# Down projection of a SwiGLU block: six of eleven pairs of row blocks as Strassen-Winograd units between the gate products

## The chip, the cores and the metric

The kernel runs on one core of a Trainium2 chip. The metric is the time of one execution in device microseconds (us). Of the kernel before there are three runs, with a median of 1959.67 us (1958.75 to 1963.95), and one execution with a profile. The engines are called as in the profile: PE (TensorE, the matmuls), PEld (its weight loads), DVE (VectorE), ACT (ScalarE), POOL (GpSimd) and SP (SyncE, which issues the loads from DRAM).

## The reference

The program is an encoder of two layers (DEPTH 2) on 512 tokens with 1024 channels, all in float32. Each layer has a SwiGLU feed-forward block (FFN), a mixer of four kinds of attention heads, and a second FFN:

```python
def _swiglu(h, w_gu, w_down):
    gate, up = jnp.split(h @ w_gu, 2, axis=-1)
    return (jax.nn.silu(gate) * up) @ w_down
...
    alpha = (2 * DEPTH) ** 0.25
    for l in range(DEPTH):
        x = _layer_norm(alpha * x + 0.5 * _swiglu(x, ffn_w_gu[l, 0], ffn_w_down[l, 0]), ln_g[l, 0], ln_b[l, 0])
        mix = _token_mixers(x, ...)
        x = _layer_norm(alpha * x + mix, ln_g[l, 1], ln_b[l, 1])
        x = _layer_norm(alpha * x + 0.5 * _swiglu(x, ffn_w_gu[l, 1], ffn_w_down[l, 1]), ln_g[l, 2], ln_b[l, 2])
```

The inner width D_FF is 2816, so w_gu is 1024 x 5632 (gate and up side by side) and w_down is 2816 x 1024. There are four FFNs in all; only they are touched here, the mixers are not.

## The kernel before

**Precision.** A float32 operand is split into a high part (a cast by ACT to a matmul type, `wh`, `hh`) and a low part (the rest, a subtraction by DVE, `wl`, `hl`). Every product is three matmuls: high by high, high by low, low by high.

**Gate and up.** The work goes by eleven pairs j = 0 to 10 (class `Pair`). A pair makes 256 columns of the gate and the 256 columns of the up projection for all tokens, as a 2 x 2 block matrix product with seven products in place of eight (Winograd's form). Its four blocks of weights `b11`, `b21`, `b12`, `b22` (128 x 1024 each) are loaded by SP and added up to the operands of the seven products; the sums of the activations `al1` to `al7` stand ready for the whole FFN. Each operand of weights is split by `parts4` (the cast at L399, the low part at L400). One product (`product`, L404 to L416) is two halves of 12 matmuls with 256 columns. The program runs them in the order 1, 2, 5, 6, 7, 3, 4 into the PSUM tiles `ga` (1, 6, 7, 4), `gb` (2) and `gc` (5, 3); between them ACT copies intermediate results (`s1`, `p5`, `u2`) and DVE adds to them, and at the end of the pair silu and two multiplications give `h0` and `h1`, the pair's two blocks of 256 inner channels for the two halves of the tokens. In pairs 0 and 1 of an FFN the order is different: products 1 and 2 of both pairs come first, since the later products need the later token blocks, which the stage before has just finished.

`prep_rest` makes four sums of weights with DVE (L442): b11 + b12 in place, `t2` = b11 + b12 + b22 in a tile of its own, b12 + b22 in place, and b21 + t2 in place. For pair 0 these sums are made while the stage before still runs, since nothing holds them back but the loads.

**Down projection.** After the last pair come 22 row blocks c (128 inner channels each). A block's weights, 128 x 1024, are loaded (`wr`), cast and split (L237, L238), and its part of h is cast and split by `h_of` (L532, L533). For each of four token blocks and two column halves, `down` (L537) runs three matmuls of 512 columns, 24 for a row block. They accumulate in all eight PSUM banks (`acc`) from c = 0 to 21. The last four row blocks (TAIL) run token block by token block, so that the layer norm of one block goes on while the next is still computed. The layer norm reads a bank and adds it, times 0.5/alpha, to x (L313), where x is the residual.

**What sets the order.** The program is one stream per engine. The framework's scheduler places the instructions of each engine, within the dependencies; pools of tiles with a fixed number of buffers per tag set how early a load or a cast can start. `h` tiles live in free buffers of the mixers' tags (HSLOTS), since all 22 of them must be there until the down projection. `gain_later` (L358) multiplies x by the gain and adds the shift of the layer norm before, for the FFNs that follow one whose normalization was left so (FFNs 2 to 4); before, it runs after pairs 2, 3, 4 and 5, one token block at each.

Of the kernel before, what the change touches and what calls it, by code (L numbers as in the profile page):

```python
# [11 lines left out]
F32 = mybir.dt.float32  # L12
F32R = mybir.dt.float32r
# [59 lines left out]
def tile_encoder(ctx: ExitStack, tc: tile.TileContext, d: dict, out: bass.AP):  # L73
# [293 lines left out]
    HSLOTS = ["oT"] * 8 + ["nat"] * 4 + ["tb"] * 3 + ["hl"] * 6 + ["v"]  # L367
    TMP = ["o", "o", "od", "o2", "o2", "kr"]

    def ffn(l, f, last, to_next):  # L370
# [3 lines left out]
        slots = list(HSLOTS)  # L374
# [43 lines left out]
        class Pair:  # L418
# [16 lines left out]
            def prep12(self, early=(None, None)):  # L435
                self.w[1] = parts4(self.r[11], early[0])
                self.w[2] = parts4(self.r[21], early[1])
                return self

            def prep_rest(self):  # L440
                r = self.r
                add = lambda o, a, b: ve.tensor_tensor(o, a, b, op=ALU.add)  # L442
                add(r[11], r[11], r[12])
                self.w[5] = parts4(r[11])
                t2 = raw_tile("t2")
                add(t2, r[11], r[22])
                self.w[6] = parts4(t2)
                add(r[12], r[12], r[22])
                self.w[7] = parts4(r[12])
                self.w[3] = parts4(r[22])  # L450
                add(r[21], r[21], t2)
                self.w[4] = parts4(r[21])
                return self

# [3 lines left out]
            def run12(self):  # L458
                self.a = self.bank("s", "ga")
                product(1, self.a, self.w[1], True)  # L460
                self.s1 = tmp("s1").rearrange("p (c t) -> p c t", c=2)
                se.copy(self.s1, self.a)
                b = self.bank("pj", "gb")
                product(2, b, self.w[2], True)

                ve.tensor_tensor(self.s1, b, self.s1, op=ALU.add)

            def run_rest(self):
                v3 = lambda t: t.rearrange("p (c t) -> p c t", c=2)
                a = self.a  # L470
                c = self.bank("pj", "gc")
                product(5, c, self.w[5], True)
                p5 = v3(tmp("p5"))
                se.copy(p5, c)
                product(6, a, self.w[6], False)
                u2 = v3(tmp("u2"))
                se.copy(u2, a)  # L477
                product(7, a, self.w[7], False)

                ve.tensor_tensor(p5, a, p5, op=ALU.add)  # L480
                product(3, c, self.w[3], False)
                se.activation(self.s1, self.s1, AF.Silu, scale=-1.0)

                ve.tensor_tensor(u2, c, u2, op=ALU.add)
                product(4, a, self.w[4], False)
                h0 = v3(block(slots.pop(0), "h0"))
                ve.tensor_tensor(h0, self.s1, u2, op=ALU.mult)
                s2 = v3(tmp("s2"))
                se.activation(s2, a, AF.Silu, scale=-1.0)
                h1 = v3(block(slots.pop(0), "h1"))  # L490
                ve.tensor_tensor(h1, s2, p5, op=ALU.mult)
                H.append((h0, h1))

        p0, p1 = Pair(0), Pair(1)
        if opening:
            opening.pop(0)()
            p0.load().prep12(("p", "nat"))
            p0.run12()
            opening.pop(0)()
# [1061 lines left out]
```

## Time and profile before

| what | value |
|---|---|
| median of three runs | 1959.67 us |
| profiled execution | 1961.2 us, span 1959.4 us |
| granted TensorE clock, mean | 0.991 |
| FFN 1: gate and up, then down | 11.0 to 248.0 us, to about 369 |
| FFN 2 | 630.5 to 864.6, to about 988 |
| FFN 3 | about 989 to 1216, to about 1337 |
| FFN 4 | 1596 to 1831.4, to about 1951 |

The times of the four FFNs are the first and last starts of the tiles `ga` and `acc` in the trace. The mixers of the two layers lie between FFN 1 and 2 and between FFN 3 and 4. A group's row in the profile reads: line of the kernel, engine, operation, tile written and tile read, shapes, count, then the busy time in us and the mean duration of one in ns, then the idle time of the engine just before these instructions and what ended it. Window rows give for a stretch of time the busy time of PE, PEld, DVE, ACT and POOL with the number of instructions, the granted clock, the share of the DMA engines and GB/s.

### The profile page before, as it was taken

The numbers are of one execution on the slowest core, as the hardware profiler recorded it, in microseconds if no ns is written. First come the engines' busy times: TensorE is split into PE (matmuls) and PEld (weight loads), VectorE is DVE, ScalarE is ACT, GpSimd is POOL, SyncE is SP. The second block draws the span as 40 slices with busy tenths as digits, with TensorE's granted clock in tenths as the row PEclk, the third lists the DMA queues.
The fourth block names the chain that finished last, engine by engine and source line by source line (L and its number), as shares of the span: only waits on it lengthen the run. The fifth ranks groups of instructions, "written<-read, shape, count | busy, mean of one in ns | idle before, by whom it ended". The sixth has DMA issues, their size and how long they took to land. (4 is left out here: it accounts for less than half of the span.)

```text
span 1959.4 us, 32008 instructions
## 1 busy us (share of the span) xinstructions
PE 1905.6 (97%) x12396; PEld 1729.8 (88%) x12396; DVE 1452.8 (74%) x2265; ACT 999.1 (51%) x1695; POOL 262.4 (13%) x387
## 2 busy tenths in 40 slices
PE   7999999999999999999999999999999989999998
PEld 7999988788778899998899999887887879999886
DVE  7887753758999998763499787437689989978535
ACT  5544442238776754453275545322587875544421
POOL 0000000235741000000000000004367300000001
PEclk9999999999999999999999999999999999999999
DMA  5333233343333333332323322331433434332321
GB/s 192 114 103 97 97 115 104 100 113 87 107 101 105 113 103 104 108 129 97 103 90 111 110 96 99 108 120 55 134 90 84 107 100 141 99 108 85 108 97 65
DMA packets 157496, 205.61 MB, mean 105 GB/s; under 512 B 14560, under 2 KB 123104, under 8 KB 157344
## 3 DMA queue, kind: packets, MB, share of 16 engines
q1 hardware_dynamic: 157344, 203.56, 33.4%
q8 instruction: 98, 1.61, 0.3%
q14 instruction: 54, 0.44, 0.1%
HBM read 178.49 MB, written 2.10 MB: 92 GB/s over the span
## 5 line engine op out<-in xcount | busy, mean ns | idle before, releaser
L399 ACT CAST wh<-b 128x1024 fp32r<-128x1024 f32 x256 | 268.2, 1050 | 292.0 <-issue 168.9
L265 PE MATMUL ga<-al,wh 128*128 128x256 f32 x2752 | 392.1, 285 | 0.3 <-ACT u L477 0.3
L400 DVE TENSOR_TENSOR wl<-b,wh 128x1024 fp32r<-128x1024 f32 x256 | 310.3, 1218 | 93.4 <-ACT wh L399 93.3
L265 PEld LDWEIGHTS ga<-al,wh 128*128 128x128 f32 x2752 | 354.4, 191 | 8.9 <-ACT u L477 8.7
L238 DVE TENSOR_TENSOR wl<-wr,wh 128x1024 fp32r<-128x1024 f32 (+1 forms) x92 | 112.2, 1220 | 228.8 <-ACT wh L237 228.8
L265 PE MATMUL acc<-wl,hh 128*128 128x512 f32 x704 | 274.7, 390 | 0.0
L265 PE MATMUL acc<-wh,hl 128*128 128x512 f32 x704 | 274.3, 390 | 0.0
L265 PE MATMUL acc<-wh,hh 128*128 128x512 f32 x704 | 274.3, 390 | 0.0
L237 ACT CAST wh<-wr 128x1024 fp32r<-128x1024 f32 (+2 forms) x98 | 101.5, 1040 | 254.7 <-PE acc L265 219.8
L265 PE MATMUL ga<-al,wl 128*128 128x256 f32 x1376 | 221.3, 283 | 0.0
L333 POOL TENSOR_TENSOR rs<-rs,mhalf 128x1 f32<-128x1 f32 x24 | 20.0, 833 | 1481.3 <-DVE rs L332 1466.8
L265 PE MATMUL gc<-al,wh 128*128 128x256 f32 x1408 | 201.0, 285 | 5.9 <-ACT al L177 4.5
L265 PEld LDWEIGHTS ga<-al,wl 128*128 128x128 f32 x1376 | 189.7, 192 | 0.2 <-DVE wl L400 0.2
L265 PEld LDWEIGHTS gc<-al,wh 128*128 128x128 f32 x1408 | 183.6, 193 | 7.0 <-ACT al L177 4.8
L265 PEld LDWEIGHTS acc<-wl,hh 128*128 128x128 f32 x704 | 132.2, 188 | 28.0 <-DVE wl L238 0.5
L265 PEld LDWEIGHTS acc<-wh,hl 128*128 128x128 f32 x704 | 132.2, 188 | 27.1
L265 PEld LDWEIGHTS acc<-wh,hh 128*128 128x128 f32 x704 | 132.2, 188 | 26.9
L265 PE MATMUL gc<-al,wl 128*128 128x256 f32 x704 | 120.0, 284 | 0.0
L442 DVE TENSOR_TENSOR b<-b,b 128x1024 f32<-128x1024 f32 x88 | 107.2, 1219 | 2.6 <-DMA b<-in_ffn_w_gu_dram 1.7
L265 PE MATMUL gb<-al,wh 128*128 128x256 f32 x640 | 93.2, 289 | 9.2 <-ACT wh L399 9.2
L265 PEld LDWEIGHTS gc<-al,wl 128*128 128x128 f32 x704 | 100.6, 193 | 0.0
L265 PEld LDWEIGHTS gb<-al,wh 128*128 128x128 f32 x640 | 85.4, 198 | 9.6 <-ACT wh L399 9.6
(293 smaller groups left out, 3408.6 us busy)
## 6 DMA issues: line engine op xcount, KB each, us to landing
b<-in_ffn_w_gu_dram SPq DMA_DIRECT2D x176, 512.0 KB, 3.4
wr<-in_ffn_w_down_dram SPq DMA_DIRECT2D x88, 512.0 KB, 3.2
wr<-in_w_in_dram SPq DMA_DIRECT2D x30, 512.0 KB, 3.7
k<-ph SPq DMA_DIRECT2D x64, 128.0 KB, 2.4
wr<-in_w_out_dram SPq DMA_DIRECT2D x16, 512.0 KB, 3.3
qs<-ph SPq DMA_DIRECT2D x32, 128.0 KB, 2.4
ln_g<-in_ln_g_dram SPq DMA_DIRECT2D x14, 256.0 KB, 5.5
ln_b<-in_ln_b_dram SPq DMA_DIRECT2D x14, 256.0 KB, 5.8
```

The costliest lines, as they stand in the source:

```text
L237: se.copy(h[:, w], r[:, w])
L238: (lo or ve).tensor_tensor(l[:, q], r[:, q], h[:, q].bitcast(F32), op=ALU.subtract)
L265: te.matmul(o, a, b, start=start, stop=stop, **kw)
L333: ge.tensor_tensor(rs[:, 1:2], rs[:, 0:1], mhalf[:, 0:1], op=ALU.pow)
L399: se.copy(h, r[:, q])
L400: ve.tensor_tensor(lo, r[:, q], h.bitcast(F32), op=ALU.subtract)
L442: add = lambda o, a, b: ve.tensor_tensor(o, a, b, op=ALU.add)
```

## The change

Pairs 0 to 5, so row blocks 0 to 11 of the down weights, no longer go through the accumulating loop. Two pairs make a unit (class `Unit`, three per FFN): four blocks of h (two pairs, two halves of the tokens) and 2 x 2 blocks of 256 x 512 of the down weights. The unit computes its 512 x 1024 result by seven products, in each of which one operand is a sum of h blocks and the other a sum of weight blocks. A product is 12 matmuls of 512 columns in two PSUM banks (`da`, `db` or `dc`). After each step DVE adds the two banks, times plus or minus 0.5/alpha, straight into the x tiles (L555 of the changed kernel). Products 3, 6, 7 and 4 go on accumulating in the banks of an earlier product, so what is added to x then is the sum.

The 21 steps of an FFN are placed between the gate products, from the first product of pair 3 on, about one step per 2.5 products, up to the 52nd. A unit's weights come in eight loads of 256 KB into buffers of the tag `hl`. `Pair` is split in one function per product, and makes its sums of weights in place, without `t2`: b11 becomes b11 + b12 and then b11 + b12 + b22 after product 5's operand has been split. The accumulating loop starts at c = 12. `gain_later` comes earlier: token blocks 0 and 1 after pair 2, 2 and 3 with the first two unit steps, since x must have its gains before a step adds to it. The tags of the `h` tiles and of their splits change (HTAGS, PARTS), because six pairs' h tiles are now free before the down loop.

```diff
-    def ffn(l, f, last, to_next):
+    HTAGS = ["oT"] * 4 + ["nat"] * 2 + ["tb"] + ["v"] * 2 + ["oT"] * 2
+    PARTS = {6: "p", 7: "oT", 8: "p", 9: "nat", 10: "v"}
+    UNITS = 3
...
+    def ffn(l, f, last, to_next, early=("p", "nat")):
...
+            def step5(self):
+                r = self.r
+                ve.tensor_tensor(r[11], r[11], r[12], op=ALU.add)
+                w = parts4(r[11])
+                self.c = self.bank("pj", "gc")
+                product(5, self.c, w, True)
...
+            def step6(self):
+                r = self.r
+                ve.tensor_tensor(r[11], r[11], r[22], op=ALU.add)
+                w = parts4(r[11])
+                product(6, self.a, w, False)
...
+        class Unit:
...
+            def load(self):
+                for n, k, u in ((11, 0, 0), (21, 1, 0), (12, 0, 1), (22, 1, 1)):
+                    self.r[n] = []
+                    for q in range(2):
+                        r = block("hl", "d")
+                        c = 2 * (self.j + k) + q
+                        load(r, wd[c * P:(c + 1) * P, u * FD:(u + 1) * FD])
+                        self.r[n].append(r)
+
+            def add(self, o, a):
+                for q in range(2):
+                    ve.tensor_tensor(self.r[o][q], self.r[o][q], self.r[a][q], op=ALU.add)
+
+            def step(self, n, h, sign, rn, banks, first, outs):
+
+                hh, hl = (block("p", "dh", F32R) for _ in range(2))
+                h = h.rearrange("p c t -> p (c t)") if len(h.shape) == 3 else h
+                if sign == 1.0:
+                    se.copy(hh, h)
+                    ve.tensor_tensor(hl, h, hh.bitcast(F32), op=ALU.subtract)
...
+                hh, hl = v3(hh), v3(hl)
+                wh = whi.tile([P, DM], F32R, tag="h", name="wh", bufs=WB)
+                wl = wlo.tile([P, DM], F32R, tag="l", name="wl", bufs=WB)
+                for q in range(2):
+                    sl = slice(q * FD, (q + 1) * FD)
+                    se.copy(wh[:, sl], self.r[rn][q])
+                    ve.tensor_tensor(wl[:, sl], self.r[rn][q], wh[:, sl].bitcast(F32), op=ALU.subtract)
+                for i in range(2):
+                    ts = slice(i * P, (i + 1) * P)
+                    seq = []
...
+                    for m, (a, b) in enumerate(seq):
+                        mm(banks[i], a, b, first and m == 0, m == len(seq) - 1, skip_group_check=True)
+                for i in range(2):
+                    half, cols, sign = outs
+                    xs = x[2 * half + i][:, cols * FD:(cols + 1) * FD]
+                    ve.scalar_tensor_tensor(xs, banks[i], sign * 0.5 * INV_A, xs, op0=ALU.mult, op1=ALU.add)
+
+            def steps(self):
...
+                self.load()
+                a = two(("pt", "pt"), "da")
+                self.step(1, h11, -1.0, 11, a, True, (0, 0, -1.0))
+                yield
+                b = two(("pv", "pj"), "db")
+                self.step(2, h12, -1.0, 21, b, True, (0, 0, -1.0))
+                yield
+                t = block("tb", "dt")
+                ve.tensor_tensor(t, h21, h22, op=ALU.subtract)
+                self.add(11, 12)
+                c = two(("pv", "pj"), "dc")
+                self.step(5, t, 1.0, 11, c, True, (1, 1, 1.0))
+                yield
+                ve.tensor_tensor(t, h11, t, op=ALU.subtract)
+                ve.tensor_tensor(h12, h12, t, op=ALU.subtract)
+                self.step(3, h12, 1.0, 22, c, False, (0, 1, 1.0))
+                yield
...
+        down_steps = itertools.chain.from_iterable(Unit(2 * u).steps() for u in range(UNITS))
+        done = 0
         for j in range(2, NB):
-            p = Pair(j).load().prep12().prep_rest()
-            p.run12()
-            p.run_rest()
-            if gained and j < 6:
-                gain_later(j - 2)
...
+            p = Pair(j).load()
+            for n, step in enumerate([p.step1, p.step2] + p.rest()):
+                step()
+                if j > 2:
+                    k = 7 * (j - 3) + n + 1
+                    while done < 7 * UNITS and done * (7 * (NB - 3) - 2) < k * 7 * UNITS:
+                        next(down_steps)
+                        done += 1
+                        if gained and done <= 2:
+                            gain_later(1 + done)
...
-        for c in range(NC - TAIL):
+        for c in range(4 * UNITS, NC - TAIL):
```

Three places show how the instructions move. The numbers behind the names are those of the tiles; the line numbers are those of each kernel's own text. The first is PE in the middle of FFN 1's gate stage, where pair 5 ends with its product 4 (`al4`) and pair 6 starts with product 1 (`al1`). Before:

```order
L265 MATMUL gc_1459<-al3_104,wl_1398 128x256 x2
L265 MATMUL ga_1406<-al4_90,wh_1402 128x256 x8
L265 MATMUL ga_1406<-al4_90,wl_1403 128x256 x4
L265 MATMUL ga_1406<-al4_90,wh_1402 128x256 x8
L265 MATMUL ga_1406<-al4_90,wl_1403 128x256 x4
L265 MATMUL ga_1634<-al1_94,wh_1601 128x256
L265 MATMUL ga_1634<-al1_95,wh_1601 128x256
L265 MATMUL ga_1634<-al1_94,wh_1601 128x256
```

In the changed kernel, with step 2 of the second unit (`db`) there:

```order
L266 MATMUL ga_1549<-al4_90,wh_1798 128x256 x8
L266 MATMUL ga_1549<-al4_90,wl_1799 128x256 x4
L266 MATMUL ga_1549<-al4_90,wh_1798 128x256 x8
L266 MATMUL ga_1549<-al4_90,wl_1799 128x256 x4
L266 MATMUL db_1832<-wh_1838,dh_1834 128x512
L266 MATMUL db_1832<-wh_1838,dh_1835 128x512
L266 MATMUL db_1832<-wh_1838,dh_1834 128x512
L266 MATMUL db_1832<-wh_1838,dh_1835 128x512
L266 MATMUL db_1832<-wl_1839,dh_1834 128x512 x2
L266 MATMUL db_1833<-wh_1838,dh_1834 128x512
...
L266 MATMUL db_1833<-wl_1839,dh_1834 128x512 x2
L266 MATMUL ga_1870<-al1_94,wh_1866 128x256
```

Between the two gate products now stand twelve matmuls of 512 columns into two banks. They read a split of h (`dh`) and split weights from the same buffers that the gate products use.

The second place is DVE in the same stretch: the splits, sums and reads of banks around the end of pair 5. Before:

```order
L400 TENSOR_TENSOR wl_1602<-b11_1593,wh_1601 128x1024
L442 TENSOR_TENSOR b11_1593<-b11_1593,b12_1597 128x1024
L442 TENSOR_TENSOR t2_1614<-b11_1593,b22_1599 128x1024
L480 TENSOR_TENSOR p5_1484<-ga_1406,p5_1484 128x512
L400 TENSOR_TENSOR wl_1606<-b21_1595,wh_1605 128x1024
L484 TENSOR_TENSOR u2_1510<-gc_1459,u2_1510 128x512
L400 TENSOR_TENSOR wl_1611<-b11_1593,wh_1610 128x1024
L487 TENSOR_TENSOR h0_1587<-s1_1431,u2_1510 128x512
L442 TENSOR_TENSOR b12_1597<-b12_1597,b22_1599 128x1024
L400 TENSOR_TENSOR wl_1617<-t2_1614,wh_1616 128x1024
L491 TENSOR_TENSOR h1_1591<-s2_1589,p5_1484 128x512
L442 TENSOR_TENSOR b21_1595<-b21_1595,t2_1614 128x1024
```

In the changed kernel:

```order
L404 TENSOR_TENSOR wl_1799<-b21_1539,wh_1798 128x1024
L555 SCALAR_TENSOR_TENSOR x0_86<-da_1741,x0_86 128x512
L523 TENSOR_TENSOR d_1735<-d_1735,d_1739 128x512
L479 TENSOR_TENSOR p5_1662<-ga_1549,p5_1662 128x512
L541 TENSOR_TENSOR wl_1839<-d_1729,wh_1838 128x512
L541 TENSOR_TENSOR wl_1839<-d_1731,wh_1838 128x512
L555 SCALAR_TENSOR_TENSOR x1_87<-da_1742,x1_87 128x512
L404 TENSOR_TENSOR wl_1867<-b11_1858,wh_1866 128x1024
L531 TENSOR_TENSOR dh_2053<-h0_1225,dh_2052 128x512
L486 TENSOR_TENSOR u2_1693<-gc_1637,u2_1693 128x512
L404 TENSOR_TENSOR wl_1898<-b21_1860,wh_1897 128x1024
L495 TENSOR_TENSOR h0_1826<-s1_1574,u2_1693 128x512
```

Sums (L523) and low parts (L541, L531) of the unit and two additions of banks into x (L555) now stand between the pair's own instructions, which keep their order.

The third place is DVE at the start of FFN 2, where the splits of the activations of the last two token blocks (`al`, `ac`, `t5`, `t7`) are mixed with the first pair's weights. Before (the sums t2_7176, b12_7033 and b21_7031 stand 33 to 40 rows above wl_7179, the low part of t2_7176 for product 6):

```order
L400 TENSOR_TENSOR wl_7115<-b21_7108,wh_7114 128x1024
L178 TENSOR_TENSOR al5_6754<-t5_7004,al5_6754 128x4x128
L219 TENSOR_TENSOR ac_6862<-ac_6862,t5_7004 128x512
L178 TENSOR_TENSOR al7_6756<-t7_6999,al7_6756 128x4x128
L224 TENSOR_TENSOR ac_6876<-ac_6876,ac_6862 128x512
L400 TENSOR_TENSOR wl_7173<-b11_7029,wh_7172 128x1024
L178 TENSOR_TENSOR al6_6755<-ac_6862,al6_6755 128x4x128
L178 TENSOR_TENSOR al3_6766<-ac_6876,al3_6765 128x2x128
L178 TENSOR_TENSOR al3_6768<-ac_6876,al3_6767 128x2x128
L466 TENSOR_TENSOR s1_7143<-gb_7145,s1_7143 128x512
L400 TENSOR_TENSOR wl_7179<-t2_7176,wh_7178 128x1024
L400 TENSOR_TENSOR wl_7184<-b12_7033,wh_7183 128x1024
```

In the changed kernel (b11_7219 is pair 0's block, overwritten in place; wl_7395 is the low part for product 6):

```order
L467 TENSOR_TENSOR b11_7219<-b11_7219,b22_7225 128x1024
L179 TENSOR_TENSOR al3_6958<-ac_7011,al3_6957 128x2x128
L490 TENSOR_TENSOR b21_7221<-b21_7221,b11_7219 128x1024
L216 TENSOR_TENSOR t5_7194<-t7_7189,a22_7184 128x512
L182 SCALAR_TENSOR_TENSOR al4_6943<-a22_7184,al4_6943 128x4x128
...
L179 TENSOR_TENSOR al3_6956<-ac_7066,al3_6955 128x2x128
L179 TENSOR_TENSOR al3_6958<-ac_7066,al3_6957 128x2x128
L404 TENSOR_TENSOR wl_7395<-b11_7219,wh_7394 128x1024
L404 TENSOR_TENSOR wl_7426<-b12_7223,wh_7425 128x1024
L404 TENSOR_TENSOR wl_7455<-b22_7225,wh_7454 128x1024
L404 TENSOR_TENSOR wl_7486<-b21_7221,wh_7485 128x1024
```

The two sums of 1024 elements for products 6 and 4 (L467 and L490) now stand among the splits of the last token blocks, and the low part for product 6 comes behind all of block 3's splits.

More of the change, by code (lines that the diff above doesn't have):

```diff
@@ L1 @@
 import collections
+import itertools
 import math
@@ L463, in run12 @@
                 b = self.bank("pj", "gb")
-                product(2, b, self.w[2], True)
+                product(2, b, w, True)
                 ve.tensor_tensor(self.s1, b, self.s1, op=ALU.add)
[L468 to L481, printed above, removed]
-                se.activation(self.s1, self.s1, AF.Silu, scale=-1.0)
[L484 to L487, printed above, removed]
+            def step5(self):
[4 more added lines that the diff above has]
+                product(5, self.c, w, True)
+                self.p5 = v3(tmp("p5"))
+                se.copy(self.p5, self.c)
@@ new lines, in step6, with step7 @@
+            def step6(self):
[3 more added lines that the diff above has]
+                product(6, self.a, w, False)
+                self.u2 = v3(tmp("u2"))
+                se.copy(self.u2, self.a)
+            def step7(self):
+                r = self.r
+                ve.tensor_tensor(r[12], r[12], r[22], op=ALU.add)
+                w = parts4(r[12])
+                product(7, self.a, w, False)
+                ve.tensor_tensor(self.p5, self.a, self.p5, op=ALU.add)
@@ new lines, in step3, with step4 @@
+            def step3(self):
+                w = parts4(self.r[22])
+                product(3, self.c, w, False)
+                se.activation(self.s1, self.s1, AF.Silu, scale=-1.0)
+                ve.tensor_tensor(self.u2, self.c, self.u2, op=ALU.add)
+            def step4(self):
+                r = self.r
+                ve.tensor_tensor(r[21], r[21], r[11], op=ALU.add)
+                w = parts4(r[21])
+                product(4, self.a, w, False)
+                tag = HTAGS[self.j]
+                h0 = v3(block(tag, "h0"))
+                ve.tensor_tensor(h0, self.s1, self.u2, op=ALU.mult)
@@ new lines, in ffn, with __init__ @@
+        class Unit:
+            def __init__(self, j):
+                self.j, self.r = j, {}
+            def load(self):
[15 more added lines that the diff above has]
+                    ve.tensor_tensor(hl, h, hh.bitcast(F32), op=ALU.subtract)
+                else:
+                    se.activation(hh, h, AF.Copy, scale=sign)
+                    ve.scalar_tensor_tensor(hl, h, sign, hh.bitcast(F32), op0=ALU.mult, op1=ALU.subtract)
+                hh, hl = v3(hh), v3(hl)
[8 more added lines that the diff above has]
+                    seq = []
+                    for q in range(2):
+                        sl = slice(q * FD, (q + 1) * FD)
+                        seq += [(hh[:, q, ts], wh[:, sl]), (hl[:, q, ts], wh[:, sl])]
+                    for q in range(2):
+                        seq.append((hh[:, q, ts], wl[:, q * FD:(q + 1) * FD]))
+                    for m, (a, b) in enumerate(seq):
[5 more added lines that the diff above has]
+            def steps(self):
+                (h11, h21), (h12, h22) = (tuple(t.rearrange("p c t -> p (c t)") for t in H[self.j + k]) for k in range(2))
+                two = lambda tags, name: [bank(t, name) for t in tags]
+                self.load()
[15 more added lines that the diff above has]
+                yield
+                self.add(11, 22)
+                self.step(6, t, 1.0, 11, a, False, (0, 1, 1.0))
+                yield
+                ve.tensor_tensor(h21, h21, h11, op=ALU.subtract)
+                self.add(12, 22)
+                self.step(7, h21, 1.0, 12, a, False, (1, 1, 1.0))
+                yield
+                self.add(21, 11)
+                self.step(4, h22, -1.0, 21, a, False, (1, 0, -1.0))
+                yield
```

78 lines of the change are left out of this document (34 added, 44 removed).

## The prediction

> **What bounds the kernel now.** I read the page's engine shares first, then the chain of waits, then the gate and down stages by windows and by the order of time.
>
> ```profile
> span 1959.4 us, 32008 instructions
> PE 1905.6 (97%) x12396; PEld 1729.8 (88%) x12396; DVE 1452.8 (74%) x2265; ACT 999.1 (51%) x1695; POOL 262.4 (13%) x387
> ...
> 26.00:248.00 222.00, 216.73 (x1761) 213.78 (x1760) 178.95 (x195) 111.99 (x144) 0.00 (x0) 0.98 0.33 103
> 248.00:349.00 101.00, 101.00 (x448) 83.62 (x447) 39.97 (x54) 33.84 (x44) 0.00 (x0) 1.00 0.34 112
> ...
> 1828.77 2.88 PE ga L265 x24
> 1831.65 119.73 PE acc L265 x528
> ```
>
> The two window rows are the first FFN's gate and up stage and most of its down stage (columns: stretch, length, PE, PEld, DVE, ACT, POOL, clock, DMA share, GB/s). TensorE is never free in either. DVE is busy for 179 of 222 us in the first and for 40 of 101 us in the second. The last two rows are the end of the chain: 24 matmuls of a gate product in 2.88 us, then one FFN's whole down projection, 528 matmuls in 119.73 us. So TensorE bounds each FFN, and DVE is a fast second in the gate stage, where the change puts more work on it.
>
> **What TensorE gives up.** Its pace in both stages:
>
> ```profile
> 151.88 1.12 PE L265 MATMUL gc<-al,wh 128*128 128x256 f32 x8
> 153.32 1.12 PE L265 MATMUL gc<-al,wh 128*128 128x256 f32 x8
> ...
> 270.59 0.39 PE L265 MATMUL acc<-wh,hh 128*128 128x512 f32 x1
> 275.12 0.39 PE L265 MATMUL acc<-wl,hh 128*128 128x512 f32 x1
> ```
>
> Half a product (12 matmuls of 256 columns) starts every 1.44 us, so a product takes 2.88 and a pair of seven 20.16 us. Between the last two rows lie 20 starts: 4.53/20 = 0.2265 us per matmul of 512 columns. A unit (two pairs, four row blocks of the down weights) took 4 x 24 = 96 of these; its seven products take 7 x 12 = 84. That is 12 x 0.2265 = 2.72 us per unit, and with three units in each of four FFNs **32.6 us**. The gate products, the mixers and the last ten row blocks keep their matmuls.
>
> **What DVE gets.** A unit's steps issue, all on 512 elements: 14 low parts of weights, 7 of h, 8 sums of weights, 4 of h and 14 updates of x out of PSUM: 47. They replace four 1024-element low parts and four of h in the down stage, where DVE idles. A pair keeps its 16 instructions: 7 low parts and 4 sums of 1024, 5 of 512.
>
> ```profile
> L400 DVE TENSOR_TENSOR wl<-b,wh 128x1024 fp32r<-128x1024 f32 x256 | 310.3, 1218 | 93.4 <-ACT wh L399 93.3
> L533 DVE TENSOR_TENSOR hl<-h,hh 128x512 fp32r<-128x512 f32 x88 | 59.4, 687 | 22.4 <-ACT hh L532 20.0 <-PE acc L265 1.6
> ...
> 38.05 3.49 DVE L400 TENSOR_TENSOR wl<-b,wh 128x1024 fp32r<-128x1024 f32 x3
> ...
> 349.48 0.68 DVE L313 SCALAR_TENSOR_TENSOR x<-acc,x 128x512 f32<-128x512 f32 x1
> 350.08 0.68 DVE L797 TENSOR_TENSOR we<-wr,we 128x512 fp32r<-128x512 f32 x1
> 350.68 0.69 DVE L315 BATCH_NORM_STATS2 bn<-x 128x6 f32<-128x512 f32 x1
> ```
>
> The groups say 1.22 and 0.69 us, but queued instructions overlap: three of 1024 elements end after 3.49, so they start (3.49 - 1.22)/2 = 1.135 us apart, and those of 512 start 0.60 apart, the read of PSUM included. I cost a full queue by these steps.
>
> The unit steps stand from pair 3's first product to the 52nd after it. TensorE: 52 x 2.88 + 3 x 84 x 0.2265 = 149.8 + 57.1 = 206.9 us. DVE: a pair is 11 x 1.135 + 5 x 0.60 = 15.5, a unit 47 x 0.60 = 28.2, so 52/7 x 15.5 + 3 x 28.2 = 199.7; FFNs 2 to 4 add eight of their sixteen gain updates (L361, L362), 4.8: 204.5. DVE needs 97 to 99% of TensorE's time, where a pair alone needed 77%. It fits, barely. In the order the low parts stand about four products ahead, and between a matmul's end, its read by DVE and the next low part lies less DVE than TensorE work, but for one place: pairs 3 to 5 of FFNs 2 and 4, where gains and unit work meet and DVE comes out about 1 us late. I take 1 us in FFNs 2, 3 and 4, **3 us**, with 0 and 4 each as ends (4 us is about what DVE is ahead there, if that is lost).
>
> The Trainium skill speaks against these steps: its page "VectorE: DVE Perf Modes", section "The DRAIN you can't avoid", says that an instruction starts only when the one before has left the pipe (and sends the reader to another section for exceptions). By it each costs its whole duration, and the sum is rival A's. The rows at 349.48 and 350.08 disagree: the second starts 0.08 us before the first ends.
>
> **ACT and DMA** stay under cover. A unit has 21 casts of 512 where it had four of 1024 and four of 512:
>
> ```profile
> L532 ACT CAST hh<-h 128x512 fp32r<-128x512 f32 x88 | 53.2, 620 | 56.3 <-PE acc L265 37.5 <-DVE h L487 11.2 <-DVE hl L533 7.2
> L237 ACT CAST wh<-wr 128x1024 fp32r<-128x1024 f32 x92 | 96.9, 1053 | 252.2 <-PE acc L265 219.8 <-issue 16.5 <-PE ga L265 7.3
> ...
> wr<-in_ffn_w_down_dram SPq DMA_DIRECT2D x88, 512.0 KB, 3.2
> SPq L93 <- DVE wl L400: 618.4, 114, 31.9
> ```
>
> At 0.62 that is 13.0 us per unit, 39 in the stretch, beside 112 of 222 us that ACT has now: no bound. The weights' bytes are the same, in loads of 256 KB for 512. On SP's queue a unit's loads wait until DVE frees the `hl` tiles, and gate loads stand behind them; SP already waits 618 us for DVE so. The tightest, pair 8's last block, stands behind four d tiles that the second unit's last step frees, and is read some 17 DVE instructions (over 10 us) later; the loads land in 3.2 us. I cost them at nothing; without that cover an FFN would lose those 3.2 us once per unit.
>
> **The start of each FFN.** The third pairwise sum is gone as a tile: r11 is overwritten in place, so product 6's sum can be made only after product 5's split, and two sums (2 x 1.135) that DVE made in an idle gap now stand among the splits of the activations.
>
> ```profile
> 36.91 1.22 DVE L400 TENSOR_TENSOR wl<-t,wh 128x1024 fp32r<-128x1024 f32 x1
> 39.26 0.64 PE L265 MATMUL ga<-al,wl 128*128 128x256 f32 x4
> ...
> 638.06 0.69 DVE L215 TENSOR_TENSOR t<-t,a 128x512 f32<-128x512 f32 x1 [1.18 <-ACT t L199]
> 646.90 2.08 PE L265 MATMUL gb<-al,wh 128*128 128x256 f32 x8 [4.59 <-ACT wh L399]
> 653.80 1.21 DVE L400 TENSOR_TENSOR wl<-t,wh 128x1024 fp32r<-128x1024 f32 x1
> 654.74 1.12 PE L265 MATMUL ga<-al,wh 128*128 128x256 f32 x8
> ...
> 990.87 0.69 DVE L215 TENSOR_TENSOR t<-t,a 128x512 f32<-128x512 f32 x1
> 1002.25 0.69 DVE L178 TENSOR_TENSOR al<-t,al 128x512 fp32r<-128x512 f32 x1
> 1002.99 1.09 PE L265 MATMUL gc<-al,wh 128*128 128x256 f32 x7 [0.64 <-DVE al L178]
> ```
>
> FFN 1: product 6's low part ends at 38.13 and is read at 39.26, so of 2.3 us more 1.1 is slack: 1.5 with the cast behind it. FFNs 2 and 4: from the first split of token block 2 (638.06) to that low part DVE took 15.7 us; in the new order there stand 18 instructions of 512 and 5 of 1024 elements and 4 quarter splits (0.33): 10.8 + 5.7 + 1.3 = 17.8, and ACT scales block 3 earlier, ahead of what DVE waits for: I take 3 us each. The wait of 4.59 us ahead of pair 1's second product goes, but what ends last is product 6, which waits for these splits. FFN 3: from 990.87 to block 3's split for product 5 it was 11.4 us, and is now 14 x 0.60 + 5 x 1.135 + 1.0 = 15.1: TensorE, which waited 0.64 there, waits 3.5 more. Together **11 us**; the ends are 0 (the old waits take it in) and 5 each, 20.
>
> **Handing over.** TensorE changes 84 times to a unit step. The nearest row is its wait for ACT's copy of product 6:
>
> ```profile
>   ACT u L477: 8.9, 45
> ```
>
> 8.9 us in 45 times, 0.2 each, at a place where the bank is read and written again at once. A unit step's bank was read some 2.5 products earlier, so I take a fraction, 0.03: **2.5 us**; the ends are 0 and 0.2 x 84 = 17.
>
> **Sum.** -32.6 + 11 + 3 + 2.5 = -16.1. The profiled execution took 1961.2 us (span 1959.4), 1.5 above the median of 1959.67: 1945 by its own time, **1944 us** beside the median. With all the lower ends 1927, with all the upper ones 1959.7 - 32.6 + 20 + 12 + 17 = 1976.
>
> **Rivals.**
> A, slower: DVE sets the pace between pairs 3 and 10. For it: 97 to 99% is asked of an engine that works strictly in order and waits for ACT's casts (93 us in the L400 row). Against: those waits fall where DVE is ahead. At full durations the stretch is 52/7 x (11 x 1.22 + 5 x 0.685) + 141 x 0.685 = 221.8 us, 14.9 over TensorE, 20.4 with gains; less 4 us of lead, 10.9 + 3 x 16.4 = 60. Then -32.6 + 11 + 60 + 2.5 = +41, 2001 us. It decides from a mean step of 0.647 us for 512 elements: there DVE's (260 or 268 steps per FFN, plus 43.7 for the longer ones) eats the other 19 us.
> B, no change: every handover costs 0.2 us and the starts 3.5 each: -32.6 + 14 + 3 + 17 = +1.4, 1961 us. For it the 45 waits above; against it that the banks were read long before.
> C, nearly all is kept: TensorE already waits 4.59 us at FFN 2's start, and that wait takes in the later splits: -32.6 + 3 = 1930 us. Against: product 6 ran without a wait behind it.
> That the order undoes the change is out: it has 144 matmuls fewer and the steps between the products.
>
> **Chances.** Forecast 0.60 (own range 1935 to 1953), A 0.18, B 0.12, C 0.10. Range: 1929 to 1972, which leaves out most of A and the best of C. No change is within 0.3%, 5.9 us, about what a measurement here can tell: faster 0.71 (forecast, C), same 0.11, slower 0.18.
>
> **What would show it.** In the new profile: a gate stretch that TensorE fills to 97% or more, with DVE over 90% there; 512-element DVE steps 0.60 apart; few waits of TensorE for `wl` from pair 3 on; product 6 of the first pair 1 to 4 us later behind its FFN's start. TensorE waiting for `wl` or for x's updates through the stretch would show A; a short gap at each change to `da`, `db` or `dc`, B. I am wrong if the stretch of the 52 products takes over 215 us, or if the starts lose more than 5 us each.

## The result, and the profile after

The changed kernel takes 1945.81 us (median of four runs, 1943.79 to 1948.64) beside 1959.64 (four runs, 1958.75 to 1963.95): a ratio of 0.9926, 95% interval 0.9907 to 0.9946. It is 13.8 us faster; 1944 was forecast. The profiled execution took 1943.79 us, with a span of 1942.0, 17.4 below the span of before. The head of its page, and two windows of FFN 1 and 2 between pair 3 and the last unit step (columns: stretch, length, PE, PEld, DVE, ACT, POOL, clock, DMA share, GB/s):

```profile
span 1942.0 us, 32394 instructions
PE 1876.5 (97%) x12252; PEld 1704.2 (88%) x12252; DVE 1697.9 (87%) x2733; ACT 1061.1 (55%) x1851; POOL 262.1 (13%) x387
...
89.00:300.00 211.00, 210.99 (x1527) 199.69 (x1526) 201.98 (x259) 111.86 (x156) 0.00 (x0) 1.00 0.30 95
700.00:911.00 211.00, 210.29 (x1522) 198.94 (x1521) 207.60 (x266) 110.40 (x154) 0.00 (x0) 1.00 0.33 104
```

TensorE fills the stretch, and DVE, which has gone from 74 to 87% of the span, is busy for 202 to 208 of 211 us there. DVE's pace in a full queue, by the order of time:

```profile
151.09 1.28 DVE L555 SCALAR_TENSOR_TENSOR x<-da,x 128x512 f32<-128x512 f32 x2
152.29 1.28 DVE L541 TENSOR_TENSOR wl<-d,wh 128x512 fp32r<-128x512 f32 x2
153.49 1.29 DVE L523 TENSOR_TENSOR d<-d 128x512 f32<-128x512 f32 x2
154.69 0.68 DVE L531 TENSOR_TENSOR dh<-dt,dh 128x512 fp32r<-128x512 f32 x1
155.30 1.21 DVE L404 TENSOR_TENSOR wl<-b,wh 128x1024 fp32r<-128x1024 f32 x1
156.43 0.68 DVE L573 TENSOR_TENSOR dt<-h,dt 128x512 f32<-128x512 f32 x1
```

Six instructions of 512 elements start within 3.60 us, 0.60 apart, with PSUM as an operand or without; the one of 1024 takes 1.13 until the next. TensorE's long waits are at the starts of FFNs 2, 3 and 4; in FFNs 2 and 3:

```profile
642.55 0.58 PE L266 MATMUL gc<-al,wh 128*128 128x256 f32 x1 [5.25 <-ACT al L178]
643.65 1.86 PE L266 MATMUL gc<-al,wh 128*128 128x256 f32 x7 [0.51 <-DVE al L179]
...
993.81 0.58 PE L266 MATMUL gc<-al,wh 128*128 128x256 f32 x1 [4.43 <-ACT al L178]
995.51 1.86 PE L266 MATMUL gc<-al,wh 128*128 128x256 f32 x7 [1.11 <-DVE al L179]
997.17 1.05 PE L266 MATMUL gc<-al,wl 128*128 128x256 f32 x4
998.02 1.91 PE L266 MATMUL gc<-al,wh 128*128 128x256 f32 x8
```

`gc` is pair 0's product 5. It waits for a cast of the activations (`al`), and after the wait eight matmuls take 1.91 us where they took 1.12. What that cast waited for in FFN 2, on DVE and then ACT:

```profile
638.50 1.22 DVE L467 TENSOR_TENSOR b<-b,b 128x1024 f32<-128x1024 f32 x1
...
639.97 1.22 DVE L490 TENSOR_TENSOR b<-b,b 128x1024 f32<-128x1024 f32 x1
641.11 0.68 DVE L216 TENSOR_TENSOR t<-t,a 128x512 f32<-128x512 f32 x1
...
641.84 0.66 ACT L178 CAST al<-t 128x512 fp32r<-128x512 f32 x1
```

The sums for products 6 and 4 run directly ahead of the step of token block 3 (L216) for which product 5's operand is waiting.

**Where the time went.** Four marks cut each FFN: its first gate matmul, ACT's copy of product 1 of pair 3 (`s<-ga`), ACT's silu of pair 10's product 4, and the end of the last `acc` matmul. For FFN 3 the second and third are, before and after:

```profile
1056.89 0.57 ACT L462 COPY s<-ga 128x512 f32<-128x512 f32 x1
...
1216.91 0.59 ACT L489 ACTIVATE s<-ga 128x512 f32<-128x512 f32 x1
```

```profile
1050.59 0.58 ACT L447 COPY s<-ga 128x512 f32<-128x512 f32 x1
...
1267.73 0.59 ACT L497 ACTIVATE s<-ga 128x512 f32<-128x512 f32 x1
```

From 160.02 to 217.14 us is 57.12 more, and the 252 matmuls of 512 columns that were added there are 252 x 0.2265 = 57.08. All differences, after less before, in us:

| part | FFN 1 | FFN 2 | FFN 3 | FFN 4 | sum | forecast |
|---|---|---|---|---|---|---|
| matmuls, 36 of 512 columns fewer each | -8.15 | -8.15 | -8.15 | -8.15 | -32.6 | -32.6 |
| start, to pair 3 | +0.5 | +3.3 | +6.0 | +3.4 | +13.2 | +11 |
| pairs 3 to 10, beyond the added matmuls | -0.1 | +0.4 | 0.0 | +0.2 | +0.5 | +5.5 |
| down stage, beyond the removed matmuls | -0.1 | +1.2 | 0.0 | -0.1 | +1.0 | 0 |

The two mixers, whose instructions are the same, differed by -1.1 and +1.7 us, and the opening by -0.1. With these the sum is -17.4, the difference of the spans. The same mixers took 257 to 262 us from kernel to kernel below, and FFN 4's start differed by 2 to 3 us between two kernels (early sums, and twice as many changes) that have the same instructions there, so a single figure of 1 or 2 us in this table is not sure.

The second and third marks are ACT's, and ACT runs its copy earlier or later beside TensorE, by up to 0.8 us. By TensorE's own marks (the last matmul of product 1 of pair 3, and the last gate matmul) the starts are +0.9, +3.2, +6.7 and +3.3, together 14.1, and pairs 3 to 10 are -0.5, +0.5, -0.6 and +0.3, together -0.4.

### The profile page after: what moved, and what is told of

It reads as the page before. It is cut to its first block, busy times and chain, and to the rows that moved or that the text cites. A ratio compares the mean times of both kernels' runs of the same rounds, so it can differ in the third digit from the quotient of the medians.

```text
span 1942.0 us, 32394 instructions
## 1 busy us (share of the span) xinstructions
PE 1876.5 (97%) x12252; PEld 1704.2 (88%) x12252; DVE 1697.9 (87%) x2733; ACT 1061.1 (55%) x1851; POOL 262.1 (13%) x387
## 4 chain that ended last, share of the span: by engine, by line
PE 83%; DVE 9%; ACT 3%; POOL 2%; DMA 1%; issue 1%; SPq 0%; DVEq 0%; ACTq 0%; POOLq 0%
PE ga L266 26%; PE gc L266 13%; PE acc L266 9%; PE da L266 7%; PE gb L266 6%; PE nat L266 6%; PE dc L266 3%; PE sc L266 2%; PE pjt L266 2%; PE pv L266 2%; PE ptb L110 2%; PE db L266 2%; PE op L266 2%; DVE p L751 1%; PE xtp L110 1%
## 5 line engine op out<-in xcount | busy, mean ns | idle before, releaser
L266 PEld LDWEIGHTS ga<-al,wh 128*128 128x128 f32 x2752 | 358.4, 192 | 16.1 <-ACT u L471 6.7
L404 DVE TENSOR_TENSOR wl<-b,wh 128x1024 fp32r<-128x1024 f32 x300 | 362.1, 1218 | 4.7 <-ACT wh L403 4.2
L540 ACT CAST wh<-d 128x512 fp32r<-128x512 f32 x168 | 98.0, 619 | 85.4 <-PE ga L266 40.8
L266 PE MATMUL acc<-wl,hh 128*128 128x512 f32 x320 | 125.3, 392 | 0.2 <-DVE wl L239 0.2
L266 PE MATMUL acc<-wh,hh 128*128 128x512 f32 x320 | 125.0, 391 | 0.0
L266 PE MATMUL acc<-wh,hl 128*128 128x512 f32 x320 | 124.9, 390 | 0.0
L239 DVE TENSOR_TENSOR wl<-wr,wh 128x1024 fp32r<-128x1024 f32 (+1 forms) x44 | 53.4, 1214 | 77.5 <-ACT wh L238 77.3
L541 DVE TENSOR_TENSOR wl<-d,wh 128x512 fp32r<-128x512 f32 x168 | 109.8, 683 | 0.3 <-ACT wh L540 0.2
L266 PE MATMUL da<-wh,dh 128*128 128x512 f32 x384 | 103.9, 392 | 0.0
L793 ACT CAST pth<-ptb 128x512 fp32r<-128x512 f32 (+2 forms) x128 | 69.8, 545 | 41.7 <-PE ptb L110 40.5
L796 DVE TENSOR_TENSOR ptl<-ptb,pth 128x512 fp32r<-128x512 f32 (+2 forms) x128 | 80.6, 630 | 7.1 <-ACT pth L793 6.6
```

Of the source, the lines that this page charges most:

```text
L239: (lo or ve).tensor_tensor(l[:, q], r[:, q], h[:, q].bitcast(F32), op=ALU.subtract)
L266: te.matmul(o, a, b, start=start, stop=stop, **kw)
L404: ve.tensor_tensor(lo, r[:, q], h.bitcast(F32), op=ALU.subtract)
L540: se.copy(wh[:, sl], self.r[rn][q])
L541: ve.tensor_tensor(wl[:, sl], self.r[rn][q], wh[:, sl].bitcast(F32), op=ALU.subtract)
L793: se.copy(b.ph, b.tb[:, b.k0:b.k1])
```

## The experiments

Medians are given; the kernel before ran beside each on the same chip (1959.85 to 1960.93).

### The pairs alone, without units

```diff
-    UNITS = 3
+    UNITS = 0
```

with the h tiles' tags and the places of the gain updates as before.

> Only the rewritten pairs (sums in place, one function per product), no units: all 22 row blocks go through the accumulating loop, h tiles lie in the tags of before, the gain updates follow pairs 2 to 5 as before. In the changed kernel's trace the first pairs of FFNs 1 to 4 came 0.5, 3.3, 7.2 and 3.3 us later than before, 14.3 together, while the stretch with the units cost its matmuls and no more. Theory: those 14.3 us come from the pairs' rewriting alone, so this kernel takes 1960 + 14 = 1974 us (1970 to 1978). Rival: part of them comes with the units (earlier gain updates, their loads on SP's queue, the tail of the down stage); then 1960 to 1967 us.

1976.88 us, ratio 1.0081 (1.0061 to 1.0101): 16.2 us slower than the kernel before. By the same marks the four starts came 2.5, 3.0, 5.5 and 3.9 us later than before, 14.9 together, and the tail of FFN 2 another 1.1. So the late starts belong to the pairs' rewriting and not to the units, which then bring 1976.9 - 1945.8 = 31.1 of the 32.6 us of their matmuls.

### Pair 0's sums made early again

```diff
+            def sums(self):
+                ...
+                add(r[11], r[11], r[12])
+                self.t2 = raw_tile("t2")
+                add(self.t2, r[11], r[22])
+                add(r[12], r[12], r[22])
+                add(r[21], r[21], self.t2)
...
+        p0.sums()
         for step in p0.rest():
```

> The changed kernel, but pair 0 of each FFN makes its four sums at once before product 5, with the third in a tile of its own as before; pairs 1 to 10 and the units stay. Theory: DVE makes these sums in its idle time ahead of the last token blocks' splits again, so the late starts go: FFNs 2 and 4 win 2 to 3.3 us each, FFN 1 0.5 to 2, FFN 3 3 to 7: 1946 - 11 = 1935 us (1932 to 1938). Rival: it is not the sums' place but ACT's order (casts between the splits) and the late norm of token block 3 that cost the time; then 1943 to 1946 us.

1928.79 us, ratio 0.9837 (0.9822 to 0.9852): 17.0 us below the changed kernel, and 32 below the kernel before beside it. Nothing else in this study is faster beyond the scatter of the runs. The starts stood at -0.2, +0.7, -0.8 and -0.1 us against those of before, and FFN 3's product 5 waits as little as it did:

```profile
984.94 1.10 PE L266 MATMUL gc<-al,wh 128*128 128x256 f32 x7 [0.64 <-DVE al L179]
985.88 0.64 PE L266 MATMUL gc<-al,wl 128*128 128x256 f32 x4
986.36 1.12 PE L266 MATMUL gc<-al,wh 128*128 128x256 f32 x8
```

The 4.43 us are gone, and so is the slow pace behind them: eight matmuls take 1.12 us. Where the sums stand is the cause of the late starts, to within 0.8 us in each FFN. The gain was larger than expected (17 for 11). Of the 15.3 us between the spans of the two profiled executions (1942.0 and 1926.7) 13.7 lie in the starts, so the loss had been larger too; the rest lies mostly in the tail of FFN 2 and in pairs 3 to 10.

### A fourth unit

```diff
-    UNITS = 3
+    UNITS = 4
```

> A fourth unit: pairs 6 and 7 too, 28 steps between the same 54 products; the accumulating loop starts at row block 16. TensorE has 12 matmuls of 512 columns less per FFN, 10.9 us in all. DVE then needs by steps of 0.60 and 1.135 us 115 + 4 x 28.2 = 228 us beside TensorE's 149.8 + 76.1 = 225.9 between pair 3's first product and the last step (gain updates: 4.8 more in FFNs 2 to 4). Theory: DVE's steps hold, so the gain is eaten by some 0 to 3 us in each FFN: 1946 - 11 + 8 = 1943 us (1936 to 1948), and DVE has no idle time left in the stretch. Rival: DVE falls behind by its whole durations (0.685 and 1.22): 254 us beside 226, over 20 us per FFN, above 2010 us. Other rival: DVE's work spreads past the stretch into the down stage and nothing is lost: 1935 us.

1947.54 us, ratio 0.9936 (0.9916 to 0.9957): nothing gained over three units (1945.81), though TensorE has 10.9 us less to do. Beyond their matmuls, pairs 3 to 10 and the down stage together took 2.0, 6.5, 4.2 and 4.1 us more than before in the four FFNs. DVE's need less TensorE's, by steps, was 228 - 225.9 = 2.1 us in FFN 1 and 6.9 in the others, so the size fits in FFNs 1 and 2; in FFNs 3 and 4 only some 60% of it was lost. FFN 2:

```profile
700.00:940.00 240.00, 236.86 (x1654) 220.95 (x1653) 236.66 (x313) 122.70 (x177) 0.00 (x0) 1.00 0.32 101
...
743.81 0.75 PE L266 MATMUL ga<-al,wl 128*128 128x256 f32 x4 [1.16 <-DVE wl L404]
...
955.03 0.74 PE L266 MATMUL acc<-wl,hh 128*128 128x512 f32 x2 [1.10 <-DVE wl L239]
```

DVE is busy for 236.7 of 240 us, and TensorE now waits for low parts, to the start of the accumulating loop. Of its five waits in that window (3.1 us) one ends on a low part, three on casts that had themselves waited for DVE's sums (2.4 to 2.5 us each), and one on ACT's copy of product 6. Three units is as much as DVE carries in this stretch.

### Four units and the early sums

> The fourth unit and pair 0's early sums together. Theory: the two gains lie in different stages and add up: t2_pair0 less the gain of u4 over the changed kernel, 1932 us if these are 11 and 3. Rival: DVE's lead at the start of the stretch is what the fourth unit lives on, and the earlier start of the products takes it away: no better than t2_pair0.

The edit is both of the last two. 1939.43 us, ratio 0.9889 (0.9873 to 0.9906): the gains do not add up. The starts are early (74.6 to 76.2 us in FFNs 1, 2 and 4, against 74.7 to 77.3 with three units and early sums), but the fourth unit makes the kernel 10.6 us slower than three units with early sums. Pairs 3 to 10 and the down stage took 17.3 us more than their matmuls in all, against 16.8 for four units without the early sums: in both the fourth unit loses more than its 10.9 us. Beside three units the profiled execution is 1.4 us slower without the early sums and 9.2 with them, and 3.8 of these 7.8 us lie in the mixers, which have the same instructions. That the earlier start takes away DVE's lead, as the rival has it, is not shown.

### The units behind the gate stage

```diff
-                if j > 2:
+                if j > NB:
...
+        for _ in range(7 * UNITS - done):
+            next(down_steps)
         gb = gain_tiles(l, 2 * f)
```

> The changed kernel with the same three units, but all 21 steps behind the last gate product and ahead of the accumulating loop, none between the gate products (all four gain updates follow pair 2). TensorE has the same matmuls. Theory: what the gate stage hides is DVE's work. The steps' matmuls take 252 x 0.2265 = 57.1 us per FFN, DVE's 141 steps of 0.60 take 84.6; some 5 us are prepared ahead. So each FFN loses about 22 us and the kernel takes 1946 + 88 = 2034 us (2015 to 2050), with TensorE waiting for low parts in the unit steps. Rival: DVE's work would be hidden there too, and the place is of no account: 1946 us.

2049.13 us, ratio 1.0452 (1.0427 to 1.0477), 103 us slower than with the steps between the products, about 26 per FFN where 22 were expected. From the end of FFN 1's gate products to the accumulating loop, with two of TensorE's waits there:

```profile
250.00:332.00 82.00, 67.79 (x259) 49.23 (x258) 77.94 (x127) 36.35 (x63) 0.00 (x0) 0.94 0.21 62
...
278.91 1.62 PE L266 MATMUL dc<-wh,dh 128*128 128x512 f32 x3 [2.46 <-ACT wh L540]
285.60 2.75 PE L266 MATMUL dc<-wh,dh 128*128 128x512 f32 x5 [2.09 <-ACT dh L530]
...
278.24 2.18 ACT L540 CAST wh<-d 128x512 fp32r<-128x512 f32 x4 [1.26 <-DVE d L523]
284.93 0.62 ACT L530 CAST dh<-h 128x512 fp32r<-128x512 f32 x1 [4.51 <-DVE h L574]
```

The 57 us of matmuls take 81, DVE is busy for 78 of 82, and the granted clock falls to 0.94. These two waits end on ACT's casts and not, as expected, on low parts; but the casts had waited for DVE, for a sum of weights (L523) and a sum of h (L574). What makes the seven products pay is that the gate stage covers their DVE work.

### The units' sums of weights on POOL

```diff
-                    ve.tensor_tensor(self.r[o][q], self.r[o][q], self.r[a][q], op=ALU.add)
+                    ge.tensor_tensor(self.r[o][q], self.r[o][q], self.r[a][q], op=ALU.add)
```

with three units, and with four, both with the early sums.

> t2_pair0 with the units' eight sums of weights (512 elements) on POOL in place of DVE. POOL is idle in the FFNs; its addition of 512 elements took 1312 ns in the mixers, so 10.5 us per unit, hidden. DVE has 24 x 0.60 = 14.4 us less per FFN. Theory: DVE did not bind with three units but for one place in FFN 3, where t2_pair0's TensorE waited 1.2 us and that stretch took 2 us longer; so 1929 - 2 = 1927 us (1925 to 1930). Rival: POOL and DVE slow each other when they run at once, and DVE's 512-element steps get longer than 0.60: 1935 us or more.

> u4_t2 with the units' sums of weights on POOL. DVE's need between pair 3's first product and the last step falls from 228 (233 with gains) by 4 x 4.8 = 19.2 to 209 (214) us beside TensorE's 225.9. Theory: what u4 and u4_t2 lost was DVE's pace alone; then the fourth unit's 12 matmuls per FFN come through: 1929 - 10.9 = 1918 us (1915 to 1923). Rival: something else stood behind u4's loss (the start of the accumulating loop right behind the last unit, the weight loads on SP's queue); then it stays above 1925 us.

1965.99 us, ratio 1.0028 (1.0018 to 1.0038), and 1978.88 us, ratio 1.0095 (1.0079 to 1.0112): 37 and 39 us slower than the same kernels with the sums on DVE. The theory fell in both. Groups of the kernel with three units, from 88 to 306 us but for POOL's row, which is of the whole span:

```profile
L537 POOL TENSOR_TENSOR d<-d 128x512 f32<-128x512 f32 x96 | 207.1, 2166 | 783.2 <-DVE wl L555 763.7 <-DMA b<-in_ffn_w_gu_dram 15.8
...
L404 DVE TENSOR_TENSOR wl<-b,wh 128x1024 fp32r<-128x1024 f32 x53 | 71.7, 1357 | 1.1 <-ACT wh L403 1.1
L569 DVE SCALAR_TENSOR_TENSOR x<-da,x 128x512 f32<-128x512 f32 x24 | 16.2, 683 | 0.1
L513 DVE TENSOR_TENSOR h<-s,p 128x512 f32<-128x512 f32 x8 | 7.7, 958 | 0.0
```

and the same three DVE groups with the sums on DVE:

```profile
L404 DVE TENSOR_TENSOR wl<-b,wh 128x1024 fp32r<-128x1024 f32 x53 | 64.4, 1218 | 0.8 <-ACT wh L403 0.6
L569 DVE SCALAR_TENSOR_TENSOR x<-da,x 128x512 f32<-128x512 f32 x24 | 16.3, 684 | 0.3 <-PE da L266 0.2
...
L513 DVE TENSOR_TENSOR h<-s,p 128x512 f32<-128x512 f32 x8 | 5.5, 685 | 0.0
```

A POOL addition takes 2166 ns where the mixers' took 1312, and DVE's instructions with two inputs from SBUF get longer, while those that read one from PSUM stay at 683. Of the DVE rows of the whole trace that show one instruction, those of 512 elements with both inputs in SBUF took 1.26 us on average while a POOL addition ran (60 of them) and 0.69 otherwise; with an input in PSUM 0.68 both times (29 and 261). Those of 1024 went from 1.22 to 1.88 (52). One run of four POOL additions in FFN 1, and DVE beside it and after it:

```profile
151.42 7.91 POOL L537 TENSOR_TENSOR d<-d 128x512 f32<-128x512 f32 x4 [42.23 <-DVE wl L555]
...
154.18 2.31 DVE L404 TENSOR_TENSOR wl<-b,wh 128x1024 fp32r<-128x1024 f32 x1
156.41 1.77 DVE L588 TENSOR_TENSOR h<-h,dt 128x512 f32<-128x512 f32 x1
158.11 2.32 DVE L404 TENSOR_TENSOR wl<-b,wh 128x1024 fp32r<-128x1024 f32 x1
160.34 0.68 DVE L569 SCALAR_TENSOR_TENSOR x<-da,x 128x512 f32<-128x512 f32 x1
```

Over all DVE rows that overlap a POOL addition, with rows of several instructions counted by their steps, DVE lost 87 us, more than the 96 x 0.60 = 58 that was moved away. Besides, a chain of four sums takes 7.9 us where DVE made it in 2.4. By TensorE's marks pairs 3 to 10 took 4.4, 13.2, 8.7 and 12.1 us longer in the four FFNs than with the sums on DVE; how much of that is the longer chain and how much DVE's lost time was not taken apart. The Trainium skill has this rule: its page "SBUF — State Buffer", section "Who interferes with whom", says that a DVE instruction with two SBUF inputs contends with a GpSimd instruction that reads SBUF, and that one with at most one SBUF input does not, outside DVE's 2-port modes. The trace agrees in both halves (0.69 to 1.26, and 0.68 both times). With four units it was the same, so that pair says nothing on whether a fourth unit could pay with less DVE work.

### Twice as many changes to a unit

```diff
                 for i in range(2):
+                    if i:
+                        yield
...
-                self.step(1, h11, -1.0, 11, a, True, (0, 0, -1.0))
+                yield from self.step(1, h11, -1.0, 11, a, True, (0, 0, -1.0))
```

and so for all seven steps, with the pacing by half steps.

> t2_pair0 with each unit step cut in two: the six matmuls of its second bank stand one or two gate products behind those of the first. The matmuls, DVE's and ACT's work are the same; TensorE changes to a unit 168 times in place of 84. Theory: a change costs next to nothing (the changed kernel's stretch with units took 56.97 to 57.51 us more than the stretch of before, for 57.08 us of matmuls), so 1929 us (1926 to 1932). Rival: each change costs up to the 0.2 us of TensorE's wait for ACT's copy of product 6, hidden in the changed kernel by waits that it takes in: 84 more changes, 1929 + 17 = 1946 us.

1928.82 us, ratio 0.9837 (0.9821 to 0.9854), the same as without the cut (1928.79). The window of FFN 1:

```profile
88.00:306.00 218.00, 218.00 (x1580) 206.25 (x1579) 206.78 (x266) 113.92 (x161) 0.00 (x0) 1.00 0.32 100
```

TensorE has no gap. A change between gate products and unit steps costs nothing that can be measured.

### Pair 1's sums too

```diff
         p1.load(gate=False)
+        p1.sums()
```

> t2_pair0 with the early sums for pair 1 too. Theory: pair 1's sums were never in the way, since its later blocks of weights are loaded only behind pair 0's products: 1929 us (1926 to 1931). Rival: the sums of pair 1 stand among pair 0's low parts too, and another 2 to 5 us come back: 1924 to 1927 us.

1929.10 us, ratio 0.9842 (0.9827 to 0.9857): no difference. Only pair 0's sums were in the way.

### All gain updates ahead of the stretch

```diff
-                        if gained and done <= 2:
-                            gain_later(1 + done)
...
-                gain_later(0)
-                gain_later(1)
+                for t in range(NT):
+                    gain_later(t)
```

> t2_pair0 with all four token blocks' gain updates behind pair 2, none in the stretch with the unit steps. In t2_pair0 the stretch of FFN 3 took 2.0 us more than its matmuls, with TensorE waiting 1.2 us where eight gain updates (4.8 us of DVE) meet unit work; in FFNs 2 and 4 nothing. Theory: those updates decide it; without them in the stretch FFN 3 wins 1 to 2 us, 1927 us (1925 to 1929). Rival: 4.8 us more of DVE ahead of the stretch take its lead away at once: FFNs 2 to 4 lose 1 to 3 us each, 1932 to 1938 us.

1928.53 us, ratio 0.9839 (0.9825 to 0.9854): no difference that can be told. In FFN 3 the wait stayed, to within a hundredth (0.68 and 0.53 with the usual gains):

```profile
1101.57 1.21 PE L266 MATMUL ga<-al,wh 128*128 128x256 f32 x8 [0.69 <-ACT wh L403]
1103.31 0.75 PE L266 MATMUL ga<-al,wl 128*128 128x256 f32 x4 [0.52 <-DVE wl L404]
```

So it is not the gain updates that make these 1.2 us, as I had also argued in the prediction for pairs 3 to 5. What stands there is pair 5's sum for product 6, at 1101.92 us in the kernel with the usual gains, 5.9 us behind the one for product 5, with DVE full between the two. Why that happens in FFN 3 alone stays open.

## Why the prediction was right, point by point

**TensorE's gain: right.** 36 matmuls fewer per FFN, 32.6 us: the stretch grew by 56.97 to 57.51 us for 57.08 us of matmuls, the down stage fell by 64.0 to 65.3 for 288 x 0.2265 = 65.2, and without the units the kernel was 31.1 us slower. Only the reading "never free" was a little strong: in the gate window of before TensorE was busy for 216.73 of 222 us.

**DVE's pace: right, and it decided rival A.** Steps of 0.60 and 1.135 us held with the queue full for over 200 us, and DVE was busy for 202 to 208 of 211 us. The sentence of the Trainium skill that was weighed there (page "VectorE: DVE Perf Modes", section "The DRAIN you can't avoid"), that the next instruction does not start until the pipe is empty, would give whole durations (0.68 and 1.22) for the steps; these instructions start earlier, which the same section says of instructions that are not held. The fourth unit shows the margin: 2 us of DVE more than TensorE was lost in FFN 1, about what the steps give. The sum "97 to 99%, it fits, barely" was exact enough to say that three units fit and four do not.

**The dense stretch: about right in sum, not FFN by FFN.** 1 us each was taken in FFNs 2, 3 and 4, for the place in pairs 3 to 5 where gains and unit work meet. In FFNs 2 and 4 it showed up, at pair 5's product 6. In FFN 2:

```profile
764.34 1.21 PE L266 MATMUL ga<-al,wh 128*128 128x256 f32 x8 [0.19 <-ACT wh L403]
766.07 0.74 PE L266 MATMUL ga<-al,wl 128*128 128x256 f32 x4 [0.52 <-DVE wl L404]
```

From pair 5's product 2 to pair 6's, TensorE took 29.63 us in FFNs 2 and 4 and 28.47 and 28.43 in FFNs 1 and 3. That is 1.2 us in each of two FFNs and nothing in FFN 3, 2.4 for the 3 forecast. The pairs of the kernel before took 20.40 to 20.41 there. The gains' part in it has no support: in the kernel with early sums it is FFN 3 that waits at this product, and there the wait stayed when they were moved out.

**Handing over: too dear, and of the wrong sign.** 2.5 us for 84 changes; twice as many cost nothing. The row that I took it from is a wait of TensorE's weight loads for ACT's copy of product 6, for a bank that is reused at once. A unit step between the products fills it: in the changed kernel it is 6.7 us in 36 times where it had been 8.9 in 45.

```profile
  ACT u L471: 6.7, 36
```

This wait was in the time of the gate products all along: a pair of before takes 20.40 us, not the 20.16 that the prediction counts from its matmuls. So the steps brought some 0.5 us per FFN in place of costing it, as FFNs 1 and 3 show (-0.5 and -0.6 by TensorE's marks; nine waits fewer of 0.24 are 2.2 us in all), and that is what hides the 2.4 us of the dense stretch in the table's row.

**The start of each FFN: the right cause, too cheap, and partly at the wrong product.** 11 us were forecast, 13.2 measured (14.1 by TensorE's marks) and 13.7 given back when pair 0's sums were made early. FFNs 2 and 4 came within 0.4 us (3.3 and 3.4 for 3), but not as told, so that the size is luck: product 6 was to wait for its low part, and it was product 5 that waited, for the cast of block 3 behind the two sums. The wait of 4.59 us ahead of pair 1's second product went, as told, and came back there as 5.25. FFN 1 lost 0.5 for 1.5. FFN 3 lost 6.0 (6.7 by TensorE's marks) for 3.5, over the 5 us that the prediction had named as a sign of being wrong: the wait at product 5 was foreseen (3.5 us more; it was 4.43 + 1.11 - 0.64 = 4.9 more), the clock behind it was not. Windows of 3 us, the changed kernel first and then the kernel before at the same product:

```profile
994.00:997.00 3.00, 1.89 (x8) 1.59 (x9) 3.00 (x5) 3.00 (x5) 0.00 (x0) 0.50 0.56 166
997.00:1000.00 3.00, 3.00 (x16) 3.00 (x16) 3.00 (x6) 1.04 (x4) 0.00 (x0) 0.50 0.91 223
1000.00:1003.00 3.00, 3.00 (x25) 3.00 (x25) 2.76 (x3) 1.50 (x2) 0.00 (x0) 0.91 0.95 311
```

```profile
1000.00:1003.00 3.00, 2.36 (x19) 2.00 (x18) 2.65 (x6) 3.00 (x7) 0.00 (x0) 1.00 0.56 176
1003.00:1006.00 3.00, 3.00 (x25) 2.92 (x25) 3.00 (x6) 3.00 (x6) 0.00 (x0) 1.00 0.54 166
```

After 4.43 us without work the granted clock is 0.50 for between six and seven us. The 23 matmuls from 995.51 to 1000.58 took 5.07 us, where 23 x 0.120 is 2.76: 2.3 us that the sum had no term for. In FFNs 2 and 4 it changed little, since the kernel before had a wait of 4.59 us there already and the slow pace behind it. The Trainium skill states the rule, page "TensorE: Matmul & The Clock Gate", section "What's actually happening": the clock halves after an idle window of about 3.4 us and comes back after about as long of work. The trace agrees on the halving (0.64 us of waiting left the clock at 1.00, 4.43 took it to 0.50); the way back took longer here, and with the units behind the gate stage waits of 2.46 and 2.09 us, shorter than that window, were followed by a slow clock too (0.62 and 0.60 in windows of 4 us). By the page's figures half a clock for 3.4 us costs 1.7 us, an estimate; 2.3 were measured.

**The rivals.** A and B fell by the rows above. C, that the old wait takes in the later splits, was half right: in FFNs 2 and 4 the new wait is only 0.7 us longer than the old one, but it does not vanish.

**ACT and DMA: right.** ACT is busy for 110 to 112 of 211 us in the stretch, and no wait of TensorE there ends on a load.

**Why the total came out.** The starts and the tail were 3 us dearer, stretch and handing over 5 us cheaper, so errors of both signs made the sum of -16.1 come out at -17.4 between the spans. The median moved by 13.8: the profiled execution of the changed kernel is the fastest of its four, and that of the kernel before is 1.5 us above its median. That 1944 lies within 2 us of the median is therefore in part luck; that TensorE keeps the 32.6 us of its matmuls and that the starts take over a third of it back is not.

## What to carry to other kernels

Fewer matmuls paid for with vector work are worth their whole time as long as the vector engine's full-queue steps, counted over the very stretch in which the work lies, stay below TensorE's; here three units were all gain, the fourth was none. Saving a temporary by overwriting in place also takes away the freedom to make a sum early: look at what stands ahead of the late arrivals at a stage's start, and price each TensorE wait of several us with the slow clock behind it. Moving elementwise work between two SBUF tiles to POOL is no relief while DVE works on SBUF pairs too.

## What the runs showed of the hardware

- POOL and DVE slow each other when both take two inputs from SBUF: POOL's addition of 512 elements took 2166 ns in place of 1312, DVE's overlapping ones 1.26 us in place of 0.69, and DVE's instructions with an input in PSUM nothing (0.68).
- A wait of TensorE of 4.4 to 5.3 us is followed by 4.5 to 6.8 us at a granted clock of 0.50, with a matmul of 256 columns every 0.21 to 0.24 us in place of 0.120; a wait of 0.64 us is not. With the units behind the gate stage, waits of 2.46 and 2.09 us were followed by slow matmuls as well (granted clock 0.62 from 278 to 282 us and 0.60 from 285 to 289).
- DVE's instructions of 512 elements last 0.68 us and start 0.60 apart in a full queue; those of 1024 last 1.22 and start 1.13 apart.
